# Mixer of an encoder layer: 16 column tiles of the input projection as 2x2 block products in a stage of their own

## The chip, the cores and the metric

One core of one Trainium2 chip runs the kernel. The metric is the device time in microseconds (us) of one execution. The core's engines are PE (matrix products, with PEld for its weight loads), DVE (vector), ACT (scalar and table functions), POOL and SP; SP issues nearly all DMA transfers here. Each engine takes its instructions in order from its own queue.

## What is computed

One encoder layer on 1024 tokens of width 1024, in float32: half-step SwiGLU feed-forward (FFN1), a mixer, and a second feed-forward (FFN2), each with residual and layer norm. The change is in the mixer. All of its projections come from one matrix w_in:

```
x <- LN1(alpha*x + 0.5*SwiGLU_1(x))
x <- LN2(alpha*x + W_out(sig(g_na)*P_na(NA(x)) + sig(g_gla)*P_gla(GLA(x))))
x <- LN3(alpha*x + 0.5*SwiGLU_2(x))

proj = h @ w_in
na_q, na_k, na_v, g_q, g_k, g_v, g_g, dlf, dlb, gate_na, gate_gla = split(proj)
y_na = neighborhood_attention(na_q, na_k, na_v, na_rpb) @ w_branch_na
y_gla = gla_bidirectional(g_q, g_k, g_v, g_g, dlf, dlb, ...) @ w_branch_gla
merged = sigmoid(gate_na) * y_na + sigmoid(gate_gla) * y_gla
return merged @ w_out
```

NA is attention of 8 heads within an 8x16 window on a 16x64 grid of tokens. GLA is a gated linear attention of 4 heads: for chunks of 64 tokens and each of two directions, a state is carried on by `state = dec * state + add` over 16 chunks; its output is normed, multiplied by silu(g_g) and projected.

## The kernel before

Activations lie with features on partitions: each of the 8 blocks of 128 features is two tiles ("halves") of 128x512 tokens. Float32 products are made of three matmuls: each operand is split into a rounded part and a rest (`split`, `load_w`: ACT writes wh, DVE wl = raw - wh), and wh·xh, wh·xl and wl·xh are added up in one PSUM bank (`mm_steps`, L111; tiles named d). A column tile of w_in (128 columns) takes 2 halves x 8 blocks x 3 matmuls, each 128x512. FFN1 computes most of its products as 2x2 blocks with seven products in place of eight (`factors`, L479, forms the seven weight combinations; `sums_of` those of the activations; `product`, L555 to L557, the matmuls; `blocks` the order).

The mixer runs in these stages, PE strictly in the order of the program (`manual_schedule` for PE), the other engines in an order that the scheduler makes from priorities and dependences:

1. `tok_major(wnv)`: v of NA, stored to vscr.
2. `qk_pair(0)`, then NA: 64 attention steps, each `na_scores` (scores s on PE, maximum on DVE, Exp on ACT), `na_transpose` and `na_values` (outputs po). They are laid among dense work by `at(time, step)` and `run`, whose clock counts 0.65 units for each k-step of three matmuls. The dense work is `spill` of gq and gk (four tiles to gqk), `decay_rank` (dls), `qk_pair(1..3)` and `tok_major(wgv)` (v of GLA). `qk_pair` computes q and k of two heads and splits them as they leave PSUM (L927 to L935).
3. GLA: for each head `gla_decay` (loads gq, gk and v; matmuls zs from dlT, L1075; logarithms, cumulative sums and exponentials on ACT and DVE, L1076 to L1097), `gla_ktrans` (kps), `gla_attn` (att), `gla_state` (matmuls sadd; copies into st, L1123 and L1124; and the recurrence in st, L1127 and L1130, 28 short DVE steps, each after the one before), `gla_out` (go reads st; then the norm, L1162 to L1174) and `gla_otrans` (opt, stored to gos). Their places are set by GLA_D0, GLA_T0, GLA_DT and GLA_OUT, and the next head's decay 12.5 units after a head's start. The dense work between them is `gate_na` of 8 tiles (a gate with Sigmoid, L1194, times the NA branch, L1197, stored to m1s) and `out_gate` of 4 (Silu, L1210).
4. `merge(j)`, 8 times: a gate_gla tile, Sigmoid, the GLA branch, and the sum with m1; then `project` and LN2.

Weights pass through two buffers "raw" and four each of "wh" and "wl"; the m1 tiles of gate_na through one buffer "hr".

Of the kernel before, what the change touches and what calls it, by code (L numbers as in the profile page):

```python
# [63 lines left out]
def hybrid_layer(ctx, tc, xT, wg1, wu1, wds1, wd1, wg2, wu2, wds2, wd2, wcol, wnv, wgv, wdl, wgate,  # L64
# [794 lines left out]
    def spill(src, m, dst, scale=1.0):  # L859
        w = load_w(src, KD * m)  # L860
        for h in range(2):
            ps = dps((m, HF))
# [41 lines left out]
    def qk_pair(p):  # L904
        wq = load_w(wcol[p], D)
        wk = load_w(wcol[4 + p], D)
# [10 lines left out]
        for h in range(2):  # L917
            hs = slice(h * HF, (h + 1) * HF)
            pq = dps()
            yield from mm_steps(pq, wq, [(blk(hi), blk(lo)) for hi, lo in x1h[h]])  # L920
# [9 lines left out]
            pk = dps()  # L930
            yield from mm_steps(pk, wk, x1h[h])
            for hh, a, o in sides:
                nc.scalar.activation(k2[hh][a, hs], pk[a], AF.Copy)
                nc.vector.tensor_copy(k2[hh][o, hs], pk[a])
# [458 lines left out]
```

## Time and profile before

| | us |
|---|---|
| median of 3 runs (2147.24 to 2150.08) | 2148.12 |
| the profiled execution | 2147.75 |
| its span | 2146.0 |
| PE busy / DVE busy / ACT busy | 2115.5 / 1349.1 / 889.6 |

The profile is of one execution. Its span runs from the first instruction to the last; the device time is 1.75 us more than it. Rows of groups read: line, engine, operation, out<-in, shape and count, then busy us, mean ns of one, and the idle time of the engine before them with what ended it. Rows of a timeline read: start, length, engine, line, operation, and in brackets idle time and its releaser. Rows of waits read: engine and line that waited, for whom, us in total, times, longest.

### The profile page before, as it was taken

What the parts mean: (1) busy time and instruction counts of PE and PEld (TensorE: products, weight loads), DVE (VectorE), ACT (ScalarE), POOL (GpSimd) and SP (SyncE); (2) the same over time, 40 slices, a digit from 0 to 9 for tenths busy, and PEclk for the clock granted to TensorE, in tenths of its full rate; (3) what the DMA queues carried; (4) which work ended last, traced back from release to release, by engine and by line L of the source; (5) the groups of instructions that cost most, each with busy time, mean ns of one, the idle gap of its engine ahead of it and who ended that gap; (6) DMA issues with size and microseconds to landing.
All of it is one profiled execution on the core that took longest, in us unless ns stands there. A gap on an engine that the chain in (4) does not pass through costs nothing.

```text
span 2146.0 us, 26727 instructions
## 1 busy us (share of the span) xinstructions
PE 2115.5 (99%) x9946; PEld 1714.7 (80%) x9946; DVE 1349.1 (63%) x2330; ACT 889.6 (41%) x1468; POOL 90.7 (4%) x85
## 2 busy tenths in 40 slices
PE   9999999999999999999999999999999999999997
PEld 7888888888887777777777788887888888888887
DVE  8667776466677254544667533489876777547647
ACT  6444444312235244446566532245544444322212
POOL 0000000000015000000000000025000000000001
PEclk9999999999999999999999999999999999999999
DMA  4434443496531322223323222322243444386732
GB/s 144 155 135 152 172 147 124 157 334 218 190 107 45 97 73 86 88 72 107 94 89 99 74 84 79 99 88 79 84 171 139 149 175 128 124 297 221 241 107 79
DMA packets 145410, 284.64 MB, mean 133 GB/s; under 512 B 15264, under 2 KB 39584, under 8 KB 145280
## 3 DMA queue, kind: packets, MB, share of 16 engines
q1 hardware_dynamic: 145280, 282.94, 39.2%
q8 instruction: 78, 1.28, 0.3%
q14 instruction: 52, 0.43, 0.1%
HBM read 199.91 MB, written 82.97 MB: 132 GB/s over the span
## 4 chain that ended last, share of the span: by engine, by line
PE 89%; DVE 7%; issue 2%; ACT 1%; DMA 1%; POOL 1%; SPq 0%; DVEq 0%; POOLq 0%; ACTq 0%
PE d L555 15%; PE d L557 15%; PE d L556 15%; PE d L118 8%; PE d L120 7%; PE d L119 7%; PE d L656 3%; PE d L655 3%; PE d L657 3%; PE d L851 1%; PE d L853 1%; PE d L852 1%; PE po L996 1%; PE pt L978 1%; PE s L961 1%
## 5 line engine op out<-in xcount | busy, mean ns | idle before, releaser
L118 PE MATMUL d<-xh,wh 128*128 128x512 f32 x640 | 260.2, 407 | 0.6 <-ACT xh L127 0.5
L119 PE MATMUL d<-xl,wh 128*128 128x512 f32 x640 | 251.4, 393 | 1.2 <-DVE xl L128 0.7
L120 PE MATMUL d<-xh,wl 128*128 128x512 f32 x640 | 251.3, 393 | 0.5 <-DVE wl L108 0.5
L127 ACT ACTIVATE wh<-raw 128x512 fp32r<-128x512 f32 (+4 forms) x132 | 98.0, 753 | 174.5 <-PE d L556 72.1
L128 DVE TENSOR_TENSOR wl<-raw,wh 128x512 fp32r<-128x512 f32 (+4 forms) x132 | 109.8, 841 | 88.9 <-ACT wh L127 88.9
L677 DVE TENSOR_TENSOR a<-a,d 128x512 f32<-128x512 f32 (+1 forms) x152 | 99.8, 656 | 89.7 <-PE d L557 59.5
L118 PEld LDWEIGHTS d<-xh,wh 128*128 128x128 f32 x640 | 120.6, 188 | 35.2 <-issue 5.5
L107 ACT ACTIVATE wh<-raw 128x512 fp32r<-128x512 f32 (+1 forms) x91 | 82.4, 907 | 146.1 <-PE d L119 90.5
L120 PEld LDWEIGHTS d<-xh,wl 128*128 128x128 f32 x640 | 120.6, 188 | 27.1 <-DVE wl L108 1.0
L119 PEld LDWEIGHTS d<-xl,wh 128*128 128x128 f32 x640 | 120.8, 189 | 26.1 <-DVE xl L128 1.6
L655 PE MATMUL d<-hh,wh 128*128 128x512 f32 (+1 forms) x368 | 134.4, 365 | 0.0
L108 DVE TENSOR_TENSOR wl<-raw,wh 128x512 fp32r<-128x512 f32 (+1 forms) x91 | 96.0, 1056 | 60.9 <-ACT wh L107 59.0
L657 PE MATMUL d<-hh,wl 128*128 128x512 f32 (+1 forms) x368 | 133.1, 362 | 0.0
L656 PE MATMUL d<-hl,wh 128*128 128x512 f32 (+1 forms) x368 | 133.1, 362 | 0.0
L555 PE MATMUL d<-a,wh 128*128 128x512 f32 x320 | 124.8, 390 | 1.6 <-DVE hr L583 1.6
L557 PE MATMUL d<-xh,wl 128*128 128x512 f32 x320 | 124.7, 390 | 0.4 <-DVE wl L128 0.4
L555 PE MATMUL d<-xh,wh 128*128 128x512 f32 x320 | 124.6, 389 | 0.0
L557 PE MATMUL d<-a,wl 128*128 128x512 f32 x320 | 124.6, 389 | 0.0
L556 PE MATMUL d<-a,wh 128*128 128x512 f32 x320 | 124.6, 389 | 0.0
L556 PE MATMUL d<-xl,wh 128*128 128x512 f32 x320 | 124.6, 389 | 0.0
L556 PE MATMUL d<-hl,hh 128*128 128x512 f32 x320 | 124.6, 389 | 0.0
L555 PE MATMUL d<-hh,hh 128*128 128x512 f32 x320 | 124.6, 389 | 0.0
(308 smaller groups left out, 4748.9 us busy)
## 6 DMA issues: line engine op xcount, KB each, us to landing
raw<-in_wu SPq DMA_DIRECT2D x44, 512.0 KB
raw<-in_wg SPq DMA_DIRECT2D x43, 512.0 KB
ops<-oh SPq DMA_DIRECT2D x84, 256.0 KB
ops<-ol SPq DMA_DIRECT2D x84, 256.0 KB
oh<-ops SPq DMA_DIRECT2D x48, 256.0 KB
ol<-ops SPq DMA_DIRECT2D x48, 256.0 KB
hid<-oh SPq DMA_DIRECT2D x40, 256.0 KB
hid<-ol SPq DMA_DIRECT2D x40, 256.0 KB
```

The lines of the kernel that those rows point to most:

```text
L118: nc.tensor.matmul(ps, a, xh, start=k == 0, stop=False)
L119: nc.tensor.matmul(ps, a, xl, start=False, stop=False)
L120: nc.tensor.matmul(ps, wl[:, k * m:(k + 1) * m], xh, start=False, stop=k == n - 1)
L127: nc.scalar.activation(hi, src, AF.Copy)
L128: nc.vector.tensor_tensor(lo, src, hi.bitcast(F32), ALU.subtract)
L555: nc.tensor.matmul(ps, a, xh, start=first and k == 0, stop=False, **sg)
L556: nc.tensor.matmul(ps, a, xl, start=False, stop=False, **sg)
L557: nc.tensor.matmul(ps, wl[:, k * P:(k + 1) * P], xh, start=False, stop=k == n - 1, **sg)
L655: nc.tensor.matmul(ps, wh, hi, start=k == 0, stop=False)
L656: nc.tensor.matmul(ps, wh, lo, start=False, stop=False)
L657: nc.tensor.matmul(ps, wl, hi, start=False, stop=k == n - 1)
L677: nc.vector.tensor_tensor(a, a, ps, ALU.add)
```

## The change

The 16 column tiles q0 to q3, k0 to k3, gq and gk (two each) and the four out gates are computed as 8 pairs of tiles in a stage of their own, `pairs`, between `tok_major(wnv)` and NA, while FFN1's buffers are still there. Each pair takes seven products of 12 matmuls. The results go to DRAM: qks, gqk, ogs (with Silu applied). `qk_pair` loads q and k back and splits them; `gla_otrans` loads the out gate and multiplies; `out_gate` only loads gos and splits it. NA now lies among `tok_major(wgv)` and six of the eight gate_gla tiles (stored to gts), GLA among `gate_na` alone, and gate_gla(0) and (1) stand ahead of `merge`, which loads m1 and gts. The constants of the order change, and the next head's decay (GLA_NEXT) stands at 7.0 in place of 12.5. v, dec, gqt and gkt of GLA get two buffers.

```diff
-GLA_D0 = 6.0
-GLA_T0 = 23.7
-GLA_DT = 31.1
-GLA_OUT = (21.4, 30.7, 30.7, 42.7)
-NA_T0 = 3.3
+GLA_D0 = 1.0
+GLA_T0 = 18.0
+GLA_DT = 24.5
+GLA_NEXT = 7.0
+GLA_OUT = (17.0, 24.0, 25.0, 32.5)
+NA_T0 = 6.0
+NA_DT = 1.45
+GATE0 = 2
...
+    def pairs(mb, items):
+        x, T = mb.x, mb.T
+        b11, b21, b22 = ([x[k + o][h] for k in range(4)] for o, h in ((0, 0), (4, 0), (4, 1)))
+
+        def store(out, h, t, src=None):
+            dst, fn, scale = out
+            if src is not None or fn != AF.Copy or scale != 1.0:
+                nc.scalar.activation(t, t if src is None else src, fn, scale=scale)
+            nc.sync.dma_start(dst[:, h * HF:(h + 1) * HF], t)
+
+        prev = None
+        for it in [*items, None]:
+            if it:
+                w = mb.factors(wcol[it[0]], wcol[it[1]])
+                X = dps()
+                yield from mb.product(X, w["a11"], b11, True)
+                s1 = mb.tmp()
+                with hoist():
+                    nc.scalar.activation(s1, X, AF.Copy)
+                Y = dps()
+                yield from mb.product(Y, w["a12"], b21, True)
+                with hoist():
+                    nc.vector.tensor_tensor(s1, Y, s1, ALU.add)
+                store(it[2], 0, s1)
+            if prev:
+                g, pX, p5, pw = prev
+                yield from mb.product(pX, pw["s3"], T[2])
+                with hoist():
+                    nc.vector.tensor_tensor(p5, pX, p5, ALU.add)
+                store(g[3], 1, p5)
+            if it:
+                Z = dps()
+                yield from mb.product(Z, w["s1"], T[0], True)
+                s5 = mb.tmp()
+                with hoist():
+                    nc.scalar.activation(s5, Z, AF.Copy)
+                yield from mb.product(X, w["s2"], T[1])
+                s2 = mb.tmp()
+                with hoist():
+                    nc.scalar.activation(s2, X, AF.Copy)
+            if prev:
+                yield from mb.product(pX, pw["a22"], T[3])
+                with hoist():
+                    store(g[3], 0, mb.tmp(), pX)
+            if it:
+                yield from mb.product(Z, w["s4"], b22)
+                with hoist():
+                    nc.vector.tensor_tensor(s2, Z, s2, ALU.add)
+                store(it[2], 1, s2)
+                prev = it, X, s5, w
...
+    x1h = [[x1[k][h] for k in range(KD)] for h in range(2)]
+    one.x, one.xr = x1, x1r
+    for i in range(4):
+        one.sums_of(i)
+    run(decay_rank())
+    plain = lambda t, scale=1.0: (t, AF.Copy, scale)
+    run(pairs(one, [(p, 4 + p, plain(qks[p], 0.125), plain(qks[4 + p])) for p in range(4)]
+              + [(8, 9, plain(gqk[0], 0.125), plain(gqk[1], 0.125)),
+                 (10, 11, plain(gqk[2]), plain(gqk[3]))]
+              + [(12 + i, 13 + i, (ogs[i], AF.Silu, 1.0), (ogs[i + 1], AF.Silu, 1.0))
+                 for i in (0, 2)]))
+    ffn1.close()
...
     def qk_pair(p):
-        wq = load_w(wcol[p], D)
-        wk = load_w(wcol[4 + p], D)
...
+        pq, pk = (wpool.tile([P, S], F32, tag="raw", name=nm("raw"), bufs=2) for _ in range(2))
+        nc.sync.dma_start(pq, qks[p])
+        nc.sync.dma_start(pk, qks[4 + p])
...
+            q4 = pq[:, hs].rearrange("p (r b c) -> p r b c", r=8, b=4)
             for hh in range(2):
                 a, o = slice(64 * hh, 64 * hh + 64), slice(64 - 64 * hh, 128 - 64 * hh)
-                t = npool.tile([P, HF], F32R, tag="q2", name=nm("q2"), bufs=4)
+                t = npool.tile([P, HF], F32R, tag="q2", name=nm("q2"), bufs=8)
                 q2[hh][h] = t
-                sides.append((hh, a, o))
-                nc.scalar.activation(t[a], pq[a], AF.Copy, scale=0.125)
-                nc.vector.scalar_tensor_tensor(t[o], pq[a], 0.125, t[a].bitcast(F32),
-                                               ALU.mult, ALU.subtract)
-            pk = dps()
-            yield from mm_steps(pk, wk, x1h[h])
-            for hh, a, o in sides:
-                nc.scalar.activation(k2[hh][a, hs], pk[a], AF.Copy)
-                nc.vector.tensor_copy(k2[hh][o, hs], pk[a])
-                nc.vector.tensor_tensor(kl[a, hs], pk[a], k2[hh][a, hs].bitcast(F32),
+                t4 = unblk(t)
...
+                nc.scalar.activation(t4[a], q4[a], AF.Copy)
+                nc.vector.tensor_tensor(t4[o], q4[a], t4[a].bitcast(F32), ALU.subtract)
+                nc.scalar.activation(k2[hh][a, hs], pk[a, hs], AF.Copy)
+                nc.vector.tensor_copy(k2[hh][o, hs], pk[a, hs])
+                nc.vector.tensor_tensor(kl[a, hs], pk[a, hs], k2[hh][a, hs].bitcast(F32),
...
-    run(qk_pair(0))
-    gl = [spill(wcol[8 + i], P, gqk[i], 0.125 if i < 2 else 1.0) for i in range(4)]
-    na_events(0, 16, NA_T0, 41)
-    run(gl[0], decay_rank(), qk_pair(1))
-    na_events(16, 32, NA_T0, 41)
-    run(gl[1], gl[2], qk_pair(2))
-    na_events(32, 48, NA_T0, 31)
-    run(gl[3], qk_pair(3))
-    na_events(48, 67, NA_T0, 41)
-    run(tok_major(wgv, lambda t: gv[t]))
+    def gate_gla(j):
+        w = load_w(wgate[KD + j], D)
+        for h in range(2):
+            ps = dps()
+            yield from mm_steps(ps, w, x1h[h])
+            sb = stage()
+            nc.scalar.activation(sb, ps, AF.Sigmoid)
+            nc.sync.dma_start(gts[j, :, h * HF:(h + 1) * HF], sb)
+
+    qk_pair(0)
+    for p in range(1, 4):
+        at(NA_T0 + (16 * p - 13) * NA_DT, lambda p=p: qk_pair(p))
+    na_events(0, 67, NA_T0, NA_T0 + 67 * NA_DT)
+    run(tok_major(wgv, lambda t: gv[t]), *[gate_gla(j) for j in range(GATE0, KD)])
...
-        nc.scalar.activation(sb, pt, AF.Copy, scale=ngt[:, 0:1])
+        nc.sync.dma_start(sb, ogs[hd, :, h * HF:(h + 1) * HF])
+        nc.vector.scalar_tensor_tensor(sb, pt, ngt[:, 0:1], sb, ALU.mult, ALU.mult)
...
     def out_gate(i):
-        w = load_w(wcol[12 + i], D)
         for h in range(2):
-            ps = dps()
-            yield from mm_steps(ps, w, x1h[h])
-            og_in = lp.tile([P, HF], F32, tag="hr", name=nm("ld"), bufs=1)
-            nc.sync.dma_start(og_in, gos[i, :, h * HF:(h + 1) * HF])
             sb = stage()
-            nc.scalar.activation(sb, ps, AF.Silu)
-            nc.vector.tensor_tensor(sb, sb, og_in, ALU.mult)
-            hi, lo = atile(F32R), atile(F32R)
-            split(sb, hi, lo)
-            og[i][h] = (hi, lo)
+            nc.sync.dma_start(sb, gos[i, :, h * HF:(h + 1) * HF])
+            og[i][h] = atile(F32R), atile(F32R)
+            split(sb, *og[i][h])
...
-            add(12.5, gla_decay, hd + 1)
+            add(GLA_NEXT, gla_decay, hd + 1)
...
-    run(*[gate_na(j) for j in range(KD)], *[out_gate(i) for i in range(4)])
-    assert not pending
+    run(*[gate_na(j) for j in range(KD)])
+    flush()
     gla.close()
+    for i in range(4):
+        out_gate(i)
...
     def merge(j):
-        wga = load_w(wgate[KD + j], D)
         wb = load_w(wbr[1, j], HF)
         for h in range(2):
-            m1 = lp.tile([P, HF], F32, tag="hr", name=nm("ld"), bufs=1)
-            nc.sync.dma_start(m1, m1s[j, :, h * HF:(h + 1) * HF])
-            pg = dps()
-            yield from mm_steps(pg, wga, x1h[h])
-            sb = stage()
-            nc.scalar.activation(sb, pg, AF.Sigmoid)
+            hs = slice(h * HF, (h + 1) * HF)
+            m1, sb = (mp.tile([P, HF], F32, tag=t, name=nm(t), bufs=3) for t in ("m1", "sb"))
+            nc.sync.dma_start(m1, m1s[j, :, hs])
+            nc.sync.dma_start(sb, gts[j, :, hs])
...
+    for j in range(GATE0):
+        run(gate_gla(j))
```

SP's queue around the weights of wgv (raw<-in_wgv). Before, in the NA stage, among attention's bias loads (bt) and the stores of gq and gk:

```order
L106 DMA raw_7474<-in_wcol 128x1024
L866 DMA gqk<-sl_6924 128x512
L951 DMA bt_7047<-in_bias 128x2x288
L951 DMA bt_7117<-in_bias 128x768
L866 DMA gqk<-sl_6990 128x512
L106 DMA raw_7832<-in_wgv 128x1024
L951 DMA bt_7241<-in_bias 128x2x288
L951 DMA bt_7341<-in_bias 128x2x288
L106 DMA raw_7838<-in_wgv 128x1024
L951 DMA bt_7402<-in_bias 128x768
L106 DMA raw_7844<-in_wgv 128x1024
```

After the change, at the end of the pairs stage (ogs stores of the last out gates; qks is the reload of k of pair 0 into "raw", vp the value loads of pair 0):

```order
L981 DMA raw_7259<-qks 128x1024
L884 DMA ogs<-hr_6990 128x512
L884 DMA gqk<-hr_6898 128x512
L884 DMA ogs<-hr_7174 128x512
L884 DMA ogs<-hr_7247 128x512
L985 DMA vp_7257<-vscr 96x1x128 x4
L985 DMA vp_7257<-vscr 128x1x128 x7
L109 DMA raw_7302<-in_wgv 128x1024
L109 DMA raw_7308<-in_wgv 128x1024
L985 DMA vp_7257<-vscr 128x1x128
L985 DMA vp_7257<-vscr 96x1x128 x4
L109 DMA raw_7314<-in_wgv 128x1024
```

The loads of wgv stood among attention steps; now all four stand behind the stores of the last products and behind the reload of q and k, whose two raw buffers they take over.

ACT's queue at the same place. Before, the first two splits of wgv (wh_7833 and wh_7839) stand between attention's Exps and read-outs:

```order
L967 ACTIVATE e_7280,sm_7281<-e_7280,sm_7281 128x288
L107 ACTIVATE wh_7833<-raw_7832 128x1024
L933 ACTIVATE k_1493_7005<-d_7258 64x512
L933 ACTIVATE k_1494_7006<-d_7258 64x512
L981 ACTIVATE et_7339<-pt_7335 96x384
```

After, d_7115 is the PSUM bank of the pairs stage's last product:

```order
L883 ACTIVATE hr_7174<-hr_7174 128x512
L883 ACTIVATE hr_7247<-d_7115 128x512
L995 ACTIVATE q_1441_7278<-raw_7258 64x8x4x16
L997 ACTIVATE k_1435_7254<-raw_7259 64x512
...
L995 ACTIVATE q_1444_7296<-raw_7258 64x8x4x16
L997 ACTIVATE k_1436_7255<-raw_7259 64x512
L110 ACTIVATE wh_7303<-raw_7302 128x1024
L110 ACTIVATE wh_7309<-raw_7308 128x1024
```

The splits of wgv now stand behind the Silu that reads the last product and behind eight copies of q and k.

DVE's queue in GLA, where the next head's decay (gz, gn, bl, gqt, gkt) meets the state recurrence of the running head (st; dec is its factor). Before, for heads 0 and 1:

```order
L1130 SCALAR_TENSOR_TENSOR st_8534<-st_8534,dec_8522 64x128
L1077 SCALAR_TENSOR_TENSOR gn_8821<-gz_8820 128x1024
L1130 SCALAR_TENSOR_TENSOR st_8534<-st_8534,dec_8522 64x128
L1197 TENSOR_TENSOR m_2024_8852<-m_2024_8852,d_8854 128x512
L1130 SCALAR_TENSOR_TENSOR st_8534<-st_8534,dec_8522 64x128 x7
L1080 SCALAR_TENSOR_TENSOR gz_8820<-gz_8820,gn_8821 128x1024
L1081 SCALAR_TENSOR_TENSOR gn_8821<-rmask,gz_8820 64x1024
L1082 SCALAR_TENSOR_TENSOR gn_8821<-rmask,gz_8820 64x1024
```

After, at the same place of a later head (L1195 and L1198 are the recurrence, L1145 to L1165 the decay):

```order
L1145 SCALAR_TENSOR_TENSOR gn_9933<-gz_9932 128x1024
...
L1148 SCALAR_TENSOR_TENSOR gz_9932<-gz_9932,gn_9933 128x1024
L1195 SCALAR_TENSOR_TENSOR st_9612<-st_9612,dec_9600 64x128
L1149 SCALAR_TENSOR_TENSOR gn_9933<-rmask,gz_9932 64x1024
L1150 SCALAR_TENSOR_TENSOR gn_9933<-rmask,gz_9932 64x1024
...
L1157 TENSOR_TENSOR gz_9932<-bl_9946,gn_9933 128x1024
L1163 TENSOR_TENSOR gkt_9951<-gkt_9951,gk_9925 128x1024
L1165 TENSOR_TENSOR gqt_9950<-gqt_9950,gq_9924 128x1024
L1160 TENSOR_TENSOR gz_9932<-gz_9932,gk_9925 128x1024
L1198 SCALAR_TENSOR_TENSOR st_9612<-st_9612,dec_9600 64x128
L1195 SCALAR_TENSOR_TENSOR st_9612<-st_9612,dec_9600 64x128
```

The next head's decay stood behind the recurrence except for its first step; now it stands ahead of 27 of the recurrence's 28 steps.

More of the change, by code (lines that the diff above doesn't have):

```diff
@@ L490, in factors @@
             with tc.high_priority(offset=HOIST):
-                nc.sync.dma_start(rg, self.wg[f])
-                nc.sync.dma_start(ru, self.wu[f])
+                nc.sync.dma_start(rg, gsrc)
+                nc.sync.dma_start(ru, usrc)
                 split(rg, *c)
@@ L567, in blocks @@
                 if f is not None:
-                    w = self.factors(f)
+                    w = self.factors(self.wg[f], self.wu[f])
                     X = dps()
@@ L818, in hybrid_layer, with to_x1, sink @@
     one = Ffn(ffn1, x, xr, half(xT), wg1, wu1, wds1, wd1, 0)
-    one.go(first, ((0, 0, HF), (1, 0, HF)), lambda h, c0, cn: to_x(x1, h))
+    x1r = [[None, None] for _ in range(KD)]
+    def to_x1(h, c0, cn):
+        put = to_x(x1, h)
+        def sink(d, y):
+            put(d, y)
+            x1r[d][h] = y
+        return sink
+    one.go(first, ((0, 0, HF), (1, 0, HF)), to_x1)
     vscr = dram.tile([S, HF], F32, tag="vscr", name="vscr")
@@ L826, in hybrid_layer @@
     m1s = dram.tile([KD, P, S], F32, tag="m1s", name="m1s")
+    qks = dram.tile([8, P, S], F32, tag="qks", name="qks")
+    ogs = dram.tile([4, P, S], F32, tag="ogs", name="ogs")
+    gts = dram.tile([KD, P, S], F32, tag="gts", name="gts")
     dls = dram.tile([32, S], F32, tag="dls", name="dls")
@@ L833, in tok_major @@
         for i in range(4):
-            if alloc is None:
+            if alloc is None or i < 2:
                 wh, wl = load_w(w_d[i], D)
@@ L857, in tok_major @@
             nc.sync.dma_start(dst(t), sb)
[L859 to L862, printed above, removed]
-            yield from mm_steps(ps, w, x1h[h])
-            sb = stage()
-            nc.scalar.activation(sb[:m], ps, AF.Copy, scale=scale)
-            nc.sync.dma_start(dst[:, h * HF:(h + 1) * HF], sb[:m])
-    run(tok_major(wnv, lambda t: vscr[t * P:(t + 1) * P, :], one.hpair))
-    assert not pending
-    ffn1.close()
@@ L871, in hybrid_layer @@
-    x1h = [[x1[k][h] for k in range(KD)] for h in range(2)]
+    def pairs(mb, items):
[46 more added lines that the diff above has]
+                prev = it, X, s5, w
@@ L893, in decay_rank @@
             nc.sync.dma_start(dls[:, h * HF:(h + 1) * HF], sb[0:32])
+    run(tok_major(wnv, lambda t: vscr[t * P:(t + 1) * P, :], one.hpair))
+    assert not pending
+    x1h = [[x1[k][h] for k in range(KD)] for h in range(2)]
[10 more added lines that the diff above has]
+    ffn1.close()
     vgrid = vscr.rearrange("(r c) e -> r c e", c=64)
@@ L1057, in hybrid_layer, with t4 @@
     heads = [dict() for _ in range(4)]
-    def t4(tag):
-        return gp.tile([P, S], F32, tag=tag, name=nm(tag))
+    def t4(tag, bufs=1):
+        return gp.tile([P, S], F32, tag=tag, name=nm(tag), bufs=bufs)
     def gla_decay(hd):
@@ L1068, in gla_decay @@
             nc.sync.dma_start(k2[half], gqk[2 + hd // 2, r])
-        v = gp.tile([P, 8, P], F32, tag="gvt", name=nm("gvt"))
+        v = gp.tile([P, 8, P], F32, tag="gvt", name=nm("gvt"), bufs=2)
         nc.sync.dma_start(v, gv[:, :, hd * P:(hd + 1) * P].rearrange("t p e -> p t e"))
@@ L1086, in gla_decay @@
         nc.vector.tensor_copy(bl[64:128], ch(nl)[64:128, :, 0])
-        dec = gp.tile([P, 16], F32, tag="dec", name=nm("dec"))
-        qt, kt = t4("gqt"), t4("gkt")
+        dec = gp.tile([P, 16], F32, tag="dec", name=nm("dec"), bufs=2)
+        qt, kt = t4("gqt", 2), t4("gkt", 2)
         nc.vector.tensor_tensor(ch(z), bl.unsqueeze(2).to_broadcast([P, 16, 64]), ch(nl),
```

8 lines of the change are left out of this document (1 added, 7 removed).

## The prediction

> **What bounds the kernel now.** I read the page first, then PE's waits, then stretches of 100 to 250 us.
>
> ```profile
> span 2146.0 us, 26727 instructions
> ...
> PE 2115.5 (99%) x9946; PEld 1714.7 (80%) x9946; DVE 1349.1 (63%) x2330; ACT 889.6 (41%) x1468; POOL 90.7 (4%) x85
> ...
> PE 89%; DVE 7%; issue 2%; ACT 1%; DMA 1%; POOL 1%; SPq 0%; DVEq 0%; POOLq 0%; ACTq 0%
> ```
>
> PE is busy for all but 30.5 us, and 89% of the chain that ended last is PE. So each matmul removed is worth its full spacing, and each new PE wait costs its full length. The waits view and a table by stretch say how little PE waits, and where:
>
> ```profile
> PE opt L1182 <- DVE on L1174: 4.4, 3, 1.9
> ...
> PE kps L1108 <- DVE gz L1092: 1.7, 1, 1.7
> ...
> PE d L555 <- DVE hr L583: 1.6, 2, 0.8
> ```
>
> ```profile
> 1260.00:1372.00 112.00, 112.00 (x496) 92.77 (x495) 41.69 (x56) 27.95 (x42) 0.00 (x0) 1.00 0.27 87
> 738.00:920.00 182.00, 182.00 (x985) 131.83 (x984) 88.42 (x238) 83.86 (x187) 0.00 (x0) 1.00 0.28 89
> 990.00:1205.00 215.00, 208.63 (x1107) 164.41 (x1107) 151.31 (x262) 129.51 (x163) 1.59 (x8) 0.98 0.33 101
> ```
>
> Columns: stretch, its length, then busy us and count of PE, PEld, DVE, ACT and POOL, PE's granted clock, DMA share, GB/s. The first row is purely dense: 112.00 / 496 = 0.226 us from one 128x512 matmul to the next, which agrees with 0.227 between neighbours in the timeline; I use 0.227. The second is the attention (NA) stage, the third GLA among the gates: even there PE is idle for only 6.4 us, though DVE is at 70%.
>
> **Step 1, matmuls removed.** 16 column tiles took 2 halves x 8 k-steps x 3 = 768 matmuls. The pairs stage has 8 pairs x 7 products x 12 = 672 of the same 128x512 size. 96 x 0.227 = **-21.8 us**. Within the stage, the products' read-outs on DVE and ACT lie beside PE work (DVE was 37% busy in the dense row). The exception is its last products: a22 accumulates onto the bank that DVE must first read after s3, the place where FFN1 shows its 0.8 us wait (d L555 <- hr L583). **+0.9.**
>
> **Step 2, the way out of the pairs stage.** PE's next work is the wgv projection. Before, its weights came in hidden between attention steps. Now the two "raw" buffers hold the reloaded q and k of pair 0 until DVE has split them, and ACT's in-order queue has the last Silu and eight 64x512 copies ahead of the first wgv split. Prices: a 512 KB load, the splits, the copies.
>
> ```profile
> 628.28 3.10 SPq L106 DMA_DIRECT2D raw<-in_wcol  x2
> ```
>
> ```profile
> 632.09 1.06 ACT L107 ACTIVATE wh<-raw 128x1024 fp32r<-128x1024 f32 x1 [1.87 <-DMA raw<-in_wcol]
> ```
>
> ```profile
> L108 DVE TENSOR_TENSOR wl<-raw,wh 128x1024 fp32r<-128x1024 f32 x12 | 14.7, 1224 | 12.5 <-ACT wh L107 12.5
> ...
> L934 DVE CAST k<-d 64x512 fp32r<-64x512 f32 x13 | 9.0, 689 | 4.9 <-ACT k L933 4.7
> ```
>
> Issue to use of a load is 632.09 - 628.28 = 3.8 us. Let E be the end of the last pair product. The Silu and eight copies at 0.6 take until about E + 5.7, DVE's last q/k split until E + 6 to 8. Then load 3.8 and split 1.06 + 1.22: the first wgv matmul starts near E + 11.5. The third and fourth weight tiles wait for the first two to leave the raw buffers and pay again, so the first 24 matmuls (5.4 us) end near E + 22 rather than E + 5.4. **+16**, bounds +10 (the copies overlap the load) and +18.
>
> **Step 3, the NA stage.** Its 64 steps now lie among 480 dense matmuls (wgv 192, gate_gla(2..7) 288) instead of some 660 between 738 and 990 us.
>
> ```profile
> L965 DVE CUSTOM_DVE_ANT_0 e<-s,bt 128x288 f32<-128x288 f32 (+1 forms) x64 | 32.3, 505 | 66.3 <-PE s L961 66.2
> L970 DVE TENSOR_SCALAR e<-e,sm 128x288 f32<-128x288 f32 (+1 forms) x64 | 25.4, 397 | 2.1
> ```
>
> ```profile
> L967 ACT ACTIVATE e<-e,sm 128x288 f32<-128x288 f32 (+1 forms) x64 | 36.9, 576 | 27.9 <-DVE sm L965 27.6
> L981 ACT ACTIVATE et<-pt 96x384 f32<-96x384 f32 (+1 forms) x64 | 31.1, 486 | 70.7 <-PE pt L978 70.6
> ...
> L967 ACT ACTIVATION_READ_ACCUMULATOR e<-e,sm 128x1 f32 x64 | 12.0, 187 | 0.0
> ```
>
> ```profile
> L1194 ACT ACT_TABLE_LOAD x12 | 15.4, 1283 | 0.2
> ...
> L1194 ACT ACTIVATE m<-d 128x512 f32<-128x512 f32 x16 | 9.5, 596 | 1.9 <-PE d L120 1.8
> ```
>
> In those 252 us some 660 dense matmuls took 150, so the 64 steps took the other 102, 1.6 each. In the new stage PE needs 480 x 0.227 + 64 x 1.6 = 211 us, 3.2 a step. ACT spends 0.58 + 0.49 + 0.19 = 1.25 a step, DVE about 1.15. New on ACT are 12 Sigmoid evictions between Exps, each with a table load in and one back: 2 x 1.28 + 0.6 = 3.2 us. All of ACT comes to 80 + 38 + some 20 for splits and copies, 138 of 211, so on average it fits; a Sigmoid block just exceeds the slack of a step now and then, and pairs 2 and 3 are split in a burst. **+4**, bounds 0 and +12.
>
> **Step 4, the entry to GLA.** The first decay's zs matmul needs dlT, which is loaded and split after the attention's last buffers come free.
>
> ```profile
> 990.04 0.88 PE L996 MATMUL po<-et,vp 96*64 96x128 f32 x12
> ...
> 999.88 0.63 PE L1075 MATMUL zs<-dlT,dec2t 96*128 96x512 f32 x2
> ```
>
> ```profile
> 993.86 0.33 SPq L857 DMA_DIRECT2D gv<-sl  x1
> ...
> 994.75 0.87 SPq L1052 DMA_DIRECT2D dlr<-dls  x2
> ```
>
> Before, 8.9 us of dense work lay between (GLA_D0 was 6.0); now 15 dense matmuls do, 3.4 us. dlT's load left at 994.75, 5.1 us ahead of zs, behind a store of gv that waited for the last wgv tile; that tile is now long done, which takes some 2 us off. I expect dlT 6.8 us after po: **+3.4**, bounds 0 and +5.5.
>
> **Step 5, the GLA outputs: the largest term.** The matmuls "go" read the states st, whose recurrence is 28 steps in a row on DVE. Before, it ended just in time:
>
> ```profile
> 1046.58 1.23 DVE L1077 SCALAR_TENSOR_TENSOR gn<-gz 128x1024 f32<-128x1024 f32 x1
> ...
> 1048.94 2.68 DVE L1130 SCALAR_TENSOR_TENSOR st<-st,dec 64x128 f32<-64x128 f32 x7
> 1051.65 1.22 DVE L1080 SCALAR_TENSOR_TENSOR gz<-gz,gn 128x1024 f32<-128x1024 f32 x1
> ```
>
> ```profile
> 1052.31 0.39 PE L1150 MATMUL go<-gvt,az 128*128 128x128 f32 x2
> ```
>
> The state chain ended at 1051.6, go started at 1052.3, and the next head's decay came behind the chain (only its first DVE step, at 1046.58, ahead). With GLA_NEXT at 7.0 the next head's zs stands 5.5 units earlier, and in the new DVE order (third pair of order rows above) the whole decay of the next head stands ahead of 27 of the 28 state steps. DVE is in order, so the chain now waits for ACT's part of the decay as well. Prices:
>
> ```profile
> L1130 DVE SCALAR_TENSOR_TENSOR st<-st,dec 64x128 f32<-64x128 f32 x56 | 19.7, 352 | 1.9
> ...
> L1124 DVE COPY st<-sadd 64x512 f32<-64x512 f32 (+1 forms) x16 | 10.4, 660 | 4.4 <-ACT st L1123 4.3
> ...
> L1081 DVE TENSOR_TENSOR_SCAN gn<-rmask,gz 64x1024 f32<-64x1024 f32 x4 | 9.1, 2283 | 0.2
> ...
> L1080 DVE SCALAR_TENSOR_TENSOR gz<-gz,gn 128x1024 f32<-128x1024 f32 x4 | 4.9, 1225 | 4.5 <-ACT gn L1079 4.4
> ...
> L1092 DVE TENSOR_TENSOR gz<-gz,gk 128x1024 f32<-128x1024 f32 x4 | 4.9, 1214 | 0.0
> ```
>
> ```profile
> L1078 ACT ACT_TABLE_LOAD x4 | 5.1, 1283 | 0.1
> ...
> L1079 ACT ACTIVATE gn<-gn 128x1024 f32<-128x1024 f32 x4 | 4.2, 1060 | 0.0
> ```
>
> ```profile
> 1033.81 1.71 PE L1118 MATMUL sadd<-gvt,ket 64*128 64x128 f32 x16
> ```
>
> From the next head's zs as zero: zs 0.6 and its two ACT copies to 2.0; first DVE step to 3.2; Exp and Ln with a table load each, 2 x (1.28 + 1.06), to 7.9; next DVE step and one state step to 9.5; two scans to 14.1; four small copies (two of 0.17, two of 0.66) to 15.8; three products to 19.5; the last waits for ACT's Exp and ends near 20.7; then 27 steps at 0.38 (2.68 / 7) = 10.3. The chain ends near **31**. PE reaches go after 45 dense matmuls (10.2), 16 sadd rows (1.7), the transposes opt and their switches: near **14.8**. Counted out by the order of each head, with the gate's read-outs that also stand between, the waits are 17, 15.4 and 14.6 us for heads 0 to 2; head 3 has no decay behind it, and there the chain itself (28 steps, sadd copies) is some 5 us late. **+52**. If DVE's copies and products slip wholly into its waits for ACT, about 13 for each of three heads remain: bound +39; above, +58.
>
> What is queued behind: the gates' m1 products on DVE. Their one buffer ("hr") is freed late, so ACT's next Sigmoid waits, and the norm of go stands behind it: opt waits some 7.0 us in all for the 4.4 of before. **+2.6.**
>
> **Step 6, after GLA.** The out gates' reload and split lie beside gate_gla(0) and (1), 22 us of PE work, which hides them. merge(j) has only its branch matmuls left, 24 x 0.227 = 5.4 us, against about 4.8 of DVE: **+1**, bounds 0 and +5; without that cover each j would cost the difference, eight times.
>
> **Step 7, the clock.** The trace shows half clock at the start, and twice for a while:
>
> ```profile
> 1.18 5.72 PE L152 MATMUL pz<-wz 128*128 128x256 bf16 x30 [1.18 <-DVE wz L149]
> ```
>
> ```profile
> 1067.50:1077.50 10.00, 10.00 (x43) 6.96 (x40) 2.68 (x4) 4.12 (x6) 0.40 (x2) 0.50 0.44 135
> ...
> 2139.50:2146.00 6.50, 0.00 (x0) 0.00 (x0) 2.58 (x3) 0.27 (x1) 1.68 (x1) 0.50 0.42 161
> ```
>
> At the start PE runs at half speed for some 4.7 us, which loses 2.3. Waits of 15 us should bring that back after each: +2.3 behind step 2, +4.6 for the two GLA waits whose loss isn't taken up by another wait. **+6.9**, bounds 0 and +10. The second stretch at half clock begins after PE's work is done; in a longer kernel it would fall on dense work, 10 us at half speed, at most 5: **+3**.
>
> The Trainium skill speaks to that: "TensorE: Matmul & The Clock Gate", section "What's actually happening", has the array's clock halve after an idle window of about 3.4 us and return after about 3.4 us of work. By that rule a restart costs 1.7 us rather than 2.3, and the sum would be 1.8 lower; but here half clock began after an idle of only 1.9 us and lasted 10 us, so the trace doesn't bear the rule out.
>
> **The sum.** -21.8 + 0.9 + 16 + 4 + 3.4 + 52 + 2.6 + 1 + 6.9 + 3 = +68. On the profiled run's own time of 2147.75 (span 2146.0), that is 2215.8; the median of the runs shown is 0.4 higher. I forecast **2215 us**. With the lower ends (-21.8 + 0.9 + 10 + 39 and nothing else) it is 2176; with the upper ones 2243.
>
> **The rivals.**
> - *Faster: DVE gets out of the way.* If the chain stood ahead of the scans or DVE did the 28 us of work in the 14.8 us that PE leaves, the GLA waits vanish, and with the reload hidden as before only -21.8 + 0.9 + some 3 is left: **2130**. For it: DVE's mean load here is 70%, and the products saved are certain. Against it: the order in the DVE queue is fixed, and 27 x 0.38 alone is 10.3 of the 14.8 us. It decides where the chain's start comes before zs + 4.5. Chance 0.05.
> - *No change: GLA fits but the reload doesn't.* -21.8 + 0.9 + 16 + 2.3 + 3.4 = +0.8: **2148.5**. The same reasons against it. Chance 0.03.
> - *Worse: ACT binds the NA stage.* If no Sigmoid block fits into a step's slack, 12 x 3.2 = 38 in place of 4: **2250**. For it: scores, Exp, transposes and Sigmoid read-outs share one in-order queue, and PE waits for each in turn. Against it: 138 us of ACT work in 211. Chance 0.10.
>
> **How the numbers follow.** My forecast has 0.82: slower. Its own bounds, cut where several would have to meet, are 2180 to 2242; leaving out both rivals below and most of the one above stays within 2 in 10. A measurement of this kernel tells about 0.2% (4.3 us) from no change. Faster 0.05, same 0.03, slower 0.92.
>
> **What would show it.** Step 1: 96 fewer dense matmuls at 0.227. Step 2: PE idle for 10 us and more ahead of the first wgv matmul, released by DVE or ACT splits of raw. Step 5: PE's largest waits are those of go for DVE's st, three near 15 us and one near 5. Step 3: waits in the NA stage that add to a few us. If go's waits are under 5 us each, the forecast is wrong at its largest term; if PE's waits in the NA stage exceed 15 us, the third rival was right.

## The result, and the profile after

The changed kernel took 2220.36 us (median of 4, 2218.26 to 2225.47) against 2148.48 us before: a ratio of 1.0338, 95% interval 1.0318 to 1.0357. A second measurement (changed_again below) gave 2221.68 and 1.0348 (1.0330 to 1.0365). It is slower by 72 us, with 96 matmuls fewer. The page of the profiled execution (2219.47 us):

```profile
span 2217.7 us, 26919 instructions
...
PE 2112.6 (95%) x9850; PEld 1705.2 (77%) x9850; DVE 1417.5 (64%) x2448; ACT 941.0 (42%) x1552; POOL 91.9 (4%) x85
...
PE 85%; DVE 8%; ACT 2%; DMA 2%; issue 1%; SPq 1%; POOL 1%; DVEq 0%; ACTq 0%; POOLq 0%
```

PE's idle time, span less busy, went from 30.5 to 105.1 us. Its busy time fell by only 2.9 us, not 21.8; the clock explains that below. The waits of PE say where it stood (line numbers are now those of the changed kernel):

```profile
PE go L1222 <- DVE st L1198: 47.4, 4, 16.3
PE d L867 <- ACT wh L110: 16.9, 2, 15.9
PE zs L1143 <- DVE dlT L1123: 3.1, 2, 1.7
PE d L121 <- ACT wh L110: 2.4, 2, 2.3
...
PE kps L1176 <- DVE gst L1253: 2.0, 3, 1.7
PE d L868 <- DVE wl L111: 1.8, 3, 0.8
PE pt L1042 <- DVE e L1034: 1.8, 2, 1.6
...
PE po L1060 <- ACT et L1045: 1.4, 3, 0.9
...
PE kps L1176 <- DVE gz L1160: 0.8, 1, 0.8
PE d L558 <- DVE hr L904: 0.8, 1, 0.8
...
PE opt L1250 <- DVE on L1242: 0.3, 1, 0.3
```

The two largest are the two that the prediction named. First the outputs of GLA. The timeline of PE for head 0, with the next head's zs and the first go:

```profile
1152.99 0.63 PE L1143 MATMUL zs<-dlT,dec2t 96*128 96x512 f32 x2
...
1167.76 0.38 PE L1218 MATMUL go<-gvt,az 128*128 128x128 f32 x2
1184.43 0.69 PE L1222 MATMUL go<-st,gqt 128*64 128x128 f32 x4 [16.29 <-DVE st L1198]
```

and that of DVE in the same stretch:

```profile
1165.00 2.29 DVE L1150 TENSOR_TENSOR_SCAN gn<-rmask,gz 64x1024 f32<-64x1024 f32 x1
...
1173.23 1.21 DVE L1165 TENSOR_TENSOR gqt<-gqt,gq 128x1024 f32<-128x1024 f32 x1
1174.48 0.35 DVE L1198 SCALAR_TENSOR_TENSOR st<-st,dec 64x128 f32<-64x128 f32 x1
...
1183.93 0.35 DVE L1198 SCALAR_TENSOR_TENSOR st<-st,dec 64x128 f32<-64x128 f32 x1
```

PE is at go 14.8 us after zs; DVE ends the decay's last product at 1174.4, starts the bulk of the recurrence at 1174.48 and ends it at 1184.28, 31.3 us after zs (24 of the 28 steps here; 27 and 26 for the next two heads). The four waits are 16.3, 13.8, 13.7 and 3.6 us.

Second the way out of the pairs stage, whose last matmul ended at 873.8. From the timelines of SP, DVE and ACT:

```profile
874.95 7.57 SPq L985 DMA_DIRECT2D vp<-vscr  x11
882.63 1.07 SPq L109 DMA_DIRECT2D raw<-in_wgv  x2
```

```profile
880.74 0.69 DVE L999 TENSOR_TENSOR kl<-raw,k 64x512 fp32r<-64x512 f32 x1
889.65 2.59 DVE L111 TENSOR_TENSOR wl<-raw,wh 128x1024 fp32r<-128x1024 f32 x2 [8.22 <-ACT wh L110]
```

```profile
888.56 1.06 ACT L110 ACTIVATE wh<-raw 128x1024 fp32r<-128x1024 f32 x1 [9.00 <-DMA raw<-in_wgv]
```

DVE let go of the raw buffers at 881.4, SP issued the weights at 882.63, behind 11 value loads, they landed 5.9 us later, and PE began at 889.7.

Third the clock. In the table by stretch, the last three figures of a row are PE's granted clock, the DMA share and GB/s:

```profile
1172.30:1192.60 20.30, 8.17 (x30) 5.56 (x31) 13.86 (x31) 2.52 (x4) 0.00 (x0) 0.50 0.37 103
1193.00:1233.00 40.00, 37.51 (x214) 29.47 (x212) 23.81 (x36) 23.89 (x32) 0.40 (x2) 1.00 0.26 86
1233.70:1254.00 20.30, 8.99 (x32) 6.21 (x33) 12.80 (x31) 2.48 (x3) 0.00 (x0) 0.50 0.33 91
1364.00:2205.00 841.00, 834.53 (x3854) 693.44 (x3853) 576.39 (x943) 323.38 (x529) 47.56 (x35) 1.00 0.45 153
```

The clock record of the trace has seven stretches at half clock between 878 and 1364 us, four that set in during the four longest waits and three at waits of 1.4 to 3.6 us. PE worked in them for 48.1 us (before: 10.2 us). Dense matmuls follow each other by 0.43 us there (at 1190.5) and by 0.23 us at full clock (at 1193.2), so this costs about half of that time: 24.0 us for 5.1. Taken off the busy times, 2112.6 - 24.0 is 21.8 less than 2115.5 - 5.1: the removed matmuls are worth just what was forecast.

### The profile page after: what moved, and what is told of

The parts are those of the page before. It is cut to its first block, busy times and chain, and to the rows that moved or that the text cites. A ratio compares the mean times of both kernels' runs of the same rounds, so it can differ in the third digit from the quotient of the medians.

```text
span 2217.7 us, 26919 instructions
## 1 busy us (share of the span) xinstructions
PE 2112.6 (95%) x9850; PEld 1705.2 (77%) x9850; DVE 1417.5 (64%) x2448; ACT 941.0 (42%) x1552; POOL 91.9 (4%) x85
## 4 chain that ended last, share of the span: by engine, by line
PE 85%; DVE 8%; ACT 2%; DMA 2%; issue 1%; SPq 1%; POOL 1%; DVEq 0%; ACTq 0%; POOLq 0%
PE d L558 17%; PE d L560 17%; PE d L559 17%; PE d L121 5%; PE d L123 5%; PE d L122 5%; PE d L659 3%; PE d L660 3%; PE d L658 3%; PE po L1060 1%; PE pt L1042 1%; DVE st L1198 1%; PE d L867 1%; PE s L1025 1%; DVE st L1195 1%
## 5 line engine op out<-in xcount | busy, mean ns | idle before, releaser
L121 PE MATMUL d<-xh,wh 128*128 128x512 f32 x384 | 160.8, 419 | 2.8 <-ACT wh L110 2.4
L122 PE MATMUL d<-xl,wh 128*128 128x512 f32 x384 | 153.3, 399 | 1.2 <-DVE xl L131 0.7
L123 PE MATMUL d<-xh,wl 128*128 128x512 f32 x384 | 153.1, 399 | 0.6 <-DVE wl L111 0.5
L558 PE MATMUL d<-a,wh 128*128 128x512 f32 x384 | 149.8, 390 | 2.4 <-DVE hr L586 1.6
L560 PE MATMUL d<-xh,wl 128*128 128x512 f32 x384 | 149.5, 389 | 0.5 <-DVE wl L131 0.5
L559 PE MATMUL d<-a,wh 128*128 128x512 f32 x384 | 149.4, 389 | 0.0
L558 PE MATMUL d<-xh,wh 128*128 128x512 f32 x384 | 149.4, 389 | 0.0
L559 PE MATMUL d<-xl,wh 128*128 128x512 f32 x384 | 149.4, 389 | 0.0
L560 PE MATMUL d<-a,wl 128*128 128x512 f32 x384 | 149.4, 389 | 0.0
L558 PE MATMUL d<-hh,hh 128*128 128x512 f32 x384 | 149.4, 389 | 0.0
L560 PE MATMUL d<-hh,hl 128*128 128x512 f32 x384 | 149.4, 389 | 0.0
L130 ACT ACTIVATE hh<-sr 128x512 fp32r<-128x512 f32 x168 | 105.9, 631 | 95.6 <-DVE sr L499 33.7
L131 DVE TENSOR_TENSOR hl<-sr,hh 128x512 fp32r<-128x512 f32 x168 | 114.2, 694 | 1.2 <-ACT hh L130 0.3
L130 ACT ACTIVATE oh<-hr 128x512 fp32r<-128x512 f32 x88 | 55.4, 631 | 128.3 <-DVE hr L587 48.4
```

The lines of the kernel that those rows point to most:

```text
L121: nc.tensor.matmul(ps, a, xh, start=k == 0, stop=False)
L122: nc.tensor.matmul(ps, a, xl, start=False, stop=False)
L123: nc.tensor.matmul(ps, wl[:, k * m:(k + 1) * m], xh, start=False, stop=k == n - 1)
L130: nc.scalar.activation(hi, src, AF.Copy)
L131: nc.vector.tensor_tensor(lo, src, hi.bitcast(F32), ALU.subtract)
L558: nc.tensor.matmul(ps, a, xh, start=first and k == 0, stop=False, **sg)
```

## The experiments

Each ratio is to the kernel before, run on the same chip with it; "half clock" is the time that PE worked at half clock in the profiled execution.

| | median us | ratio (95%) | span us | half clock us |
|---|---|---|---|---|
| the change | 2220.36 | 1.0338 (1.0318 to 1.0357) | 2217.7 | 48.1 |
| changed_again | 2221.68 | 1.0348 (1.0330 to 1.0365) | 2220.4 | 54.6 |
| next_late | 2210.48 | 1.0305 (1.0283 to 1.0327) | 2213.4 | 66.6 |
| own_buffers | 2205.37 | 1.0279 (1.0261 to 1.0297) | 2204.0 | 45.0 |
| vp_other_queue | 2212.47 | 1.0312 (1.0283 to 1.0341) | 2209.4 | 47.1 |
| filled_waits | 2214.07 | 1.0319 (1.0297 to 1.0340) | 2213.2 | 38.3 |
| old_pace | 2172.41 | 1.0112 (1.0093 to 1.0131) | 2162.4 | 29.8 |
| old_pace_next_early | 2194.90 | 1.0224 (1.0209 to 1.0239) | 2193.1 | 44.5 |
| all_mended | 2147.07 | 1.0007 (0.9997 to 1.0016) | 2143.4 | 20.6 |
| mended_out_early | 2154.44 | 1.0039 (1.0025 to 1.0053) | 2151.2 | 33.4 |
| more_mended | 2131.27 | 0.9931 (0.9914 to 0.9947) | 2138.4 | 27.3 |

The profiled execution of old_pace was its fastest (2164.14 of 2164.14 to 2173.73), those of next_late and of more_mended their slowest (2215.17 of 2207.93 to 2215.17, 2140.17 of 2127.61 to 2140.17). vp_other_queue ran twice, the others four to eleven times. In the kernels with buffers for q and k, and behind the added matmuls of filled_waits, line numbers are three higher from there on.

**The order of decay and recurrence alone (next_late).**

```diff
-GLA_NEXT = 7.0
+GLA_NEXT = 12.5
```

> Only GLA_NEXT is set back from 7.0 to 12.5, so the next head's decay is emitted behind the state recurrence; the pace (GLA_DT 24.5) and all else stay as in the change. My theory (the decay stands ahead of 27 recurrence steps on DVE): the go waits shrink from 47.4 us in all to 12 to 20 (3 to 5 for each head, since go follows sadd closely), but the decay now ends later than the next kps is due, which brings kps waits of some 6 us for each of heads 1 to 3. All PE waits of GLA together fall from 50 to 30 to 38 us, the time to 2198 to 2210. Rival A (the pace alone: DVE has too much to do at 24.5 units a head whatever its order): the waits only change their name, 45 to 55 us in all, time 2213 to 2226. Rival B (the order alone): waits under 8 us in all, time 2150 to 2165.

PE's waits:

```profile
PE go L1222 <- DVE st L1198: 16.3, 4, 5.0
PE opt L1250 <- DVE on L1242: 10.9, 4, 4.2
PE kps L1176 <- DVE gst L1253: 7.0, 2, 3.5
```

The go waits fell as expected from the order. But at this pace 11 us came back at opt, since the late decay's steps now stand among those of the norm, and 7 at kps. GLA's waits (with zs, 3.1) fell from 53.6 to 37.3 us, as expected in sum; the time, 2210.48, stayed just above the expected 2198 to 2210. In the profiled execution the clock took a part back: PE did 52.2 us of GLA's work at half clock, for 36.1 in the change, though half clock lasted for less there (61.4 us, for 71.7): at a long wait much of it falls on the wait itself, at waits of 2 to 5 us most of it falls on work. So it is neither the order alone nor the pace alone: both rivals fail.

**The raw buffers (own_buffers).**

```diff
-        pq, pk = (wpool.tile([P, S], F32, tag="raw", name=nm("raw"), bufs=2) for _ in range(2))
-        nc.sync.dma_start(pq, qks[p])
-        nc.sync.dma_start(pk, qks[4 + p])
+        half = {}
+        for h in range(2):
+            for o in (0, 4):
+                half[h, o] = npool.tile([P, HF], F32, tag="pqk", name=nm("pqk"), bufs=3)
+                nc.sync.dma_start(half[h, o], qks[o + p, :, h * HF:(h + 1) * HF])
...
```

> q and k are reloaded into three half-size buffers of their own, in place of the two raw buffers; the value loads vp stay on SP. My theory (the two raw buffers hold q and k until DVE has split them, so that the weights of wgv come late): the weights are loaded and split during the last products, the 15.9 us wait before the first wgv matmul falls to 0 to 2 us, the half clock after it goes too (2.8 us), and the time falls by 15 to 19, to 2201 to 2206. Rival (ACT's queue, with the last Silu and the copies of q and k, or SP's vp loads hold the weights back): a wait of 8 us or more stays, and the time falls by less than 10.

The wait for wh is gone from the list. But q and k now come later themselves: their loads left SP at 877.15, some 3 us after the stage's last matmul. I put that to the new buffers, which lie where FFN1's were; no run tests it. Two waits in NA took back a part:

```profile
PE go L1225 <- DVE st L1201: 47.4, 4, 16.3
PE s L1026 <- DVE k L1001: 6.5, 1, 6.5
PE pt L1045 <- DVE e L1037: 5.3, 2, 4.1
```

The half clock did not go either: behind the two waits in NA PE worked 8.0 us at half clock, behind the one for wh in the change 5.6. The time is within the expected 2201 to 2206; the ratio fell by 0.0059, 12.7 us, a little less than the expected 15 to 19 (by changed_again's ratio 14.8).

**SP's value loads (vp_other_queue).**

```diff
-                nc.sync.dma_start(vp[:4 * w, 4 * b + g, :],
+                nc.gpsimd.dma_start(vp[:4 * w, 4 * b + g, :],
```

> The value loads vp leave SP for the POOL queue; q and k still pass through the raw buffers. In the profile of the changed kernel SP issued vp loads from 874.95 to 882.52 and the weights of wgv at 882.63, while DVE let go of the raw buffers at 881.4, so both stand in the way. My theory (the raw buffers alone suffice): the weights are issued some 1 us sooner and land perhaps 1 to 2 us sooner, the wait before the first wgv matmul is 12 to 15 us, and the time falls by 1 to 4. Rival (the vp loads on SP make the wait): the wait falls by 7 us or more.

```profile
PE d L867 <- ACT wh L110: 12.2, 2, 11.9
```

Some 12 of 16 us stay while q and k hold the raw buffers: the buffers are the main cause, and the value loads on SP (0.69 us each) add 4 us to it. The span fell by 8.3 us, more than this wait did: gone too is the 2.4 us wait for a gate's weights (d L121 <- wh), whose load had stood behind seven value loads on SP, 5.5 us from 1014.36. With two executions the ratio's interval overlaps the change's, so this rests on the traces.

**Are the half clocks the waits' doing? (filled_waits)** The added matmuls are no part of the layer; go overwrites what they write.

```diff
+        if h == 0 and hd < 3:
+            for _ in range(110):
+                nc.tensor.matmul(po[:, :HF // 2], wz[:, :P], wz, start=True, stop=True)
```

> Before the first go of heads 0 to 2, PE gets 110 matmuls of 256 columns on constants into go's own bank (which go then overwrites): 110 x 0.11 = 12 us of work that fits into the waits of 13.7 to 16.3 us. My theory (the clock halves after each of these waits, and PE then worked 8.3, 9.1 and 6.4 us at half clock behind them, which loses half of that): the state recurrence ends when it did before, the three stretches of half clock there vanish, and the time falls by 8 to 12 us, to 2208 to 2213. Rival (half clock comes by time or by other waits): the stretches stay, the time is within 3 us of the changed kernel's or above it.

```profile
PE go L1225 <- DVE st L1198: 11.3, 4, 4.3
```

With 12 us of each wait filled, the end of the recurrence stayed at 31.3 us after zs, and the work at half clock behind the three waits went from 23.8 to 13.7 us. It did not vanish: 4.3, 1.7 and 1.7 us of the waits were left, and each still brought one stretch, of 6.8, 3.4 and 3.4 us, where the change had 20.5, 20.5 and 17.1. Half the difference of the whole record, (48.1 - 38.3) / 2 = 4.9, is about what the span lost (4.5). So the time, 2214.07, fell by less than the expected 8 to 12; but shorter waits made shorter stretches at the same places, and the rival, that the stretches stay, fails.

**Order and pace, two by two (old_pace, old_pace_next_early).** Beside the buffers of own_buffers:

```diff
-GLA_D0 = 1.0
-GLA_T0 = 18.0
-GLA_DT = 24.5
-GLA_NEXT = 7.0
-GLA_OUT = (17.0, 24.0, 25.0, 32.5)
-NA_T0 = 6.0
-NA_DT = 1.45
-GATE0 = 2
+GLA_D0 = 6.0
+GLA_T0 = 23.7
+GLA_DT = 31.1
+GLA_NEXT = 12.5
+GLA_OUT = (21.4, 30.7, 30.7, 42.7)
+NA_T0 = 14.0
+NA_DT = 1.02
+GATE0 = 4
...
-    run(*[gate_na(j) for j in range(KD)])
+    run(*[gate_na(j) for j in range(KD)], *[gate_gla(j) for j in range(GATE0)])
     flush()
...
-    for j in range(GATE0):
-        run(gate_gla(j))
```

old_pace_next_early is the same with GLA_NEXT at 7.0.

> The change with its three costly places undone together: q and k come back through buffers of their own, NA starts later (NA_T0 14, its steps 1.02 apart, so that the split of q and k is done), and GLA has the constants of before (GLA_DT 31.1, next decay at 12.5, GLA_D0 6.0), for which two more gate_gla tiles are moved into GLA (four there, none between GLA and merge). Nothing is computed differently. My theory (the pairs stage itself is worth -21.8 + 0.9, and all else was waits and the half clock behind them): GLA's waits are 5 to 8 us as before, go waits under 2, NA waits 2 to 6, half clock on no more than 10 to 20 us of work, the time 14 to 20 us below the kernel before (ratio 0.990 to 0.9935). Rival (the stores and reloads of the pairs stage, or DVE's additions in GLA, cost on their own): the time is within 5 us of the kernel before or above it.

> As old_pace, but with the next head's decay at 7.0 as in the change. It completes a two by two of order and pace. My theory (the decay ahead of the recurrence makes the wait, and the slower pace only moves go 4.4 units, 4.6 us, later): go waits of 7 to 12 us for heads 0 and 1, 2 to 10 for head 2, none for head 3, 20 to 32 us in all, and 5 to 9 us of half clock more, so 25 to 40 us slower than old_pace. Rival (the pace alone): go waits under 5 us in all, within 5 us of old_pace.

> The changed kernel itself, beside the others of this call on the same chip, so that they are compared with it there: span 2214 to 2222 us, go waits 47 us in all, some 105 us at half clock with PE busy for 45 to 50 of them.

changed_again gave the expected span (2220.4) and go waits (47.3), but 54.6 us of work at half clock in place of 45 to 50. The waits of old_pace, without one for go:

```profile
PE d L121 <- ACT a L130: 11.9, 4, 3.6
PE opt L1253 <- DVE on L1245: 8.8, 3, 3.5
PE pt L1045 <- DVE e L1037: 7.2, 3, 6.4
PE pt L1045 <- DVE sm L1036: 2.4, 1, 2.4
```

and the first of old_pace_next_early:

```profile
PE go L1225 <- DVE st L1201: 32.4, 3, 11.7
```

The go waits two by two, in us:

| | decay at 7.0 | decay at 12.5 |
|---|---|---|
| new pace | 47.4 | 16.3 |
| old pace | 32.4 | none |

So the order is worth 31 to 32 us of go waits at either pace, and the pace 15 to 16 in either order: the two add up, and the order is the larger. Against that, opt waits 0.3 us or not at all with the early decay and 10.9 and 8.8 with the late one. At the old pace the early decay also costs 7.4 us of half clock, and the ratio rises by 0.0112, 24 us, just short of the expected 25 to 40.

old_pace missed its expectation by far. New waits at the start of NA (9.6 us) and at merge (11.9, for the reloaded outputs, where I had taken all the cover away) gave back what the pairs stage saved. In NA, attention's first bias load stood behind 16 value loads on SP (the last 11 are shown), and DVE waited for it:

```profile
883.95 7.10 SPq L987 DMA_DIRECT2D vp<-vscr  x11
891.10 0.95 SPq L873 DMA_DIRECT2D gv<-sl  x2
892.09 0.99 SPq L1018 DMA_DIRECT2D bt<-in_bias  x2
```

```profile
896.99 0.46 DVE L1032 CUSTOM_DVE_ANT_0 e<-s,bt 128x288 f32<-128x288 f32 x1 [7.78 <-DMA bt<-in_bias]
```

**Mending those (all_mended, mended_out_early, more_mended).** all_mended is old_pace with the value loads on POOL's queue, and

```diff
-GLA_OUT = (21.4, 30.7, 30.7, 42.7)
+GLA_OUT = (21.4, 34.0, 34.0, 46.0)
-NA_DT = 1.02
-GATE0 = 4
+NA_DT = 0.86
+GATE0 = 5
...
-        at(NA_T0 + (16 * p - 13) * NA_DT, lambda p=p: qk_pair(p))
+        at(NA_T0 + (16 * p - 9) * NA_DT, lambda p=p: qk_pair(p))
...
-    run(*[gate_na(j) for j in range(KD)], *[gate_gla(j) for j in range(GATE0)])
+    run(*[gate_na(j) for j in range(KD)], *[gate_gla(j) for j in range(4)])
...
+    for j in range(4, GATE0):
+        run(gate_gla(j))
```

mended_out_early has GLA_OUT as in old_pace. more_mended is all_mended and

```diff
-NA_T0 = 14.0
-NA_DT = 0.86
+NA_T0 = 21.0
+NA_DT = 0.76
...
+    at(136.0, lambda: [out_gate(i) for i in range(3)])
...
-        add(1, gla_ktrans, hd, 1)
+        add(2.6, gla_ktrans, hd, 1)
...
-    for i in range(4):
-        out_gate(i)
+    out_gate(3)
```

> old_pace with the three waits that were left in it taken on: the value loads vp go by the POOL queue (in old_pace attention's first bias load stood behind 16 of them on SP, 0.64 us each, and PE waited 6.4 and 2.4 us); the second output of a GLA head and the transposes of the first stand at 34.0 in place of 30.7, those of the second at 46.0 (opt waited 8.8 us for the norm on DVE); one more gate_gla tile (GATE0 5) stands between GLA and merge, which waited 11.9 us for the reloaded outputs' split. My theory (all that the change lost are such waits and the half clock behind them): PE's waits fall from 46 to 22 to 28 us, about those of the kernel before, half clock falls from 30 us of PE work to 5 to 15, and the time is 10 to 20 us below the kernel before (ratio 0.990 to 0.9955). Rival (a smaller gain stage by stage, since ACT or DVE are then behind by their work and the waits only move): PE's waits stay above 35 us and the time is not below the kernel before.

> As all_mended, but the outputs of a GLA head stand as in the kernel before (30.7, 30.7, 42.7). My theory: opt waits 7 to 10 us in three waits of about 3, which bring 5 to 9 us of half clock each or between them; 8 to 16 us slower than all_mended. Rival (the later places only move the wait to kps or att of the next head): within 3 us of all_mended.

> all_mended (span 2143.4, PE idle 44.9 us in all against 30.5 in the kernel before, half clock on 20.6 us of PE work against 10.2) with its three left waits taken on: NA starts at 21.0 in steps of 0.76, so that the splits of q and k of two pairs are done on DVE (pt waited 4.7); the second kps of a head stands 2.6 units after the first in place of 1 (kps waited 6.2 for ACT's copy of the first); the out gates of heads 0 to 2 are reloaded within GLA, at 136 units, since the reload passes through two buffers and merge waited 4.8 for it. My theory (waits and the half clock that they bring are all that is left): PE idle falls to 30 to 36 us, half clock to 5 to 14 us of PE work, and the time to 2128 to 2138, 0.4 to 0.9% below the kernel before. Rival (waits only move on, since the 21.8 us of PE work were cover that DVE and ACT need): within 0.2% of all_mended and of the kernel before.

all_mended took the time of the kernel before, not the expected 10 to 20 us less: its rival was right so far. Its waits (44.9 us idle for 30.5) and half clock ate all but 2 of the 21.8 us in the profiled execution.

```profile
PE kps L1179 <- ACT ket L1181: 6.2, 3, 2.7
PE pt L1045 <- DVE e L1037: 5.9, 4, 4.6
PE d L121 <- ACT a L130: 4.8, 2, 2.5
```

The early outputs cost 0.0032, 7 us, a little under the expected 8 to 16; three opt waits, 8.8 us in all, are back there. In more_mended the waits at kps and merge are gone, and those at pt are six, of 2.4 us at most:

```profile
span 2138.4 us, 26956 instructions
...
PE 2100.3 (98%) x9850; PEld 1699.3 (79%) x9850; DVE 1416.4 (66%) x2448; ACT 934.0 (44%) x1546; POOL 135.1 (6%) x149
```

```profile
PE pt L1045 <- DVE e L1037: 5.8, 6, 2.4
...
PE opt L1253 <- ACT ket L1181: 2.1, 3, 0.7
```

It beats both kernels: 0.69% below the one before (0.53 to 0.86), some 4% below the change. That is 15 of the 21.8 us, and within the expected time. Its slowest execution, the profiled one, has 38.2 us idle and 27.3 at half clock, above the expected 30 to 36 and 5 to 14; the half clock cost it 13.7 us, 8.5 more than the kernel before.

## Why the prediction was right, step by step

- **Step 1** (-21.8 + 0.9): right. PE's work, freed of the half clock, fell by 21.8; the new wait for s3's read-out is 0.8 (d L558 <- hr L904).
- **Step 2** (+16): right in size, 16.9 + 1.8, and in its main cause. Its shape was off: I had the first matmul at 11.5 us after the stage's end and the rest of the loss in the third and fourth tile; measured are 15.9 at once and 2.8 after that. Left out was SP's part, 11 value loads ahead of the weights, which vp_other_queue put at 4 us.
- **Step 3** (+4): 1.8 + 1.4 at pt and po, and 2.4 at a gate_gla weight behind value loads on SP, which I had not named. The Sigmoid blocks did not bind ACT: the third rival fell.
- **Step 4** (+3.4): 3.1.
- **Step 5** (+52, the largest term): 47.4. The first head came out as worked out, chain end 31.3 and PE 14.8 us after zs, PE's figure in part by luck: I counted one group of sadd (1.7) and the opt transposes, but PE's way to that go has two groups (1.7 and 2.0) and no opt. It waited 16.3 for the forecast 17; heads 1 and 2 waited 13.8 and 13.7 for the forecast 15.4 and 14.6, head 3 3.6 for 5.0.
- **opt** (+2.6): wrong, -4.1. The place failed, "What is queued behind". In the kernel before, the next head's decay stands among the steps of the norm on DVE; moved ahead of the recurrence, it is done before go, and opt finds its norm ready (0.3 us in all). The two by two shows the same: opt waits for more than 0.3 us only with the late decay. kps took 1.1 more.
- **Step 6** (+1): no such wait. The cover of 22 us held.
- **Step 7** (+6.9 + 3): the mechanism was right, its size was not: (48.1 - 10.2) / 2 = 19.0 in all. I let a restart cost 2.3 us; behind the waits for go PE worked 6.4 to 9.1 us at half clock, and waits near 2 us brought it too. The other part, that the second stretch is due by time and would fall on dense work, was wrong: it began at 2209.9, 4.2 us after PE's last matmul, as it began 5.3 us after it in the kernel before. In all twelve profiles it begins 2.2 to 5.3 us after PE's last matmul, wherever that lies: it goes with the idle end, not with time.

The sum of what was measured is -21.8 + 0.8 + 18.7 + 5.6 + 3.1 + 47.4 - 4.1 + 1.1 + 19.0 = 69.8 of 71.7; the rest is in many small waits. The forecast of +68 was near in part by luck: the clock's 9 us too little stood against 11 too much at go and opt.

On the clock rule of the Trainium skill ("TensorE: Matmul & The Clock Gate", "What's actually happening") I wrote that the trace did not bear it out. That was too hard: the half-clock stretches here last 6.83, 17.07 and 20.48 us, which are 2, 5 and 6 windows of the 3.413 us it states. What the runs don't agree with is the wait it asks for, a whole idle window: stretches began at waits of 1.7 and 2.3 us.

## What to carry to other kernels

Where PE is busy nearly all the time, a count of matmuls is the smaller half of such a change: the work removed was also the cover under which other engines did theirs, and where it goes, their chains need room elsewhere before the gain shows. Read each in-order queue at the place where a step is moved, what now stands ahead of the long chain that a later matmul needs, and count in time from one common event. And price a wait of PE with the half clock behind it: here between a sixth and a third of a wait of 14 to 16 us (5.6 to 9.1 us of work at half clock behind each), and for some waits of 1.4 to 3.6 us about as much as the wait itself or several times that (in more_mended's NA stage 10.2 us of work at half clock, 5.1 us lost, behind a wait of 1.4).
